# A hybrid Hyena/mLSTM encoder layer: the stores ahead of attention move from the SyncE queue to the GpSimd queue, and one landing tile is added

## The chip, the cores and the metric

One core of a Trainium2 chip. The time is device microseconds of one execution. Engines are named as the profile names them: PE is the matrix engine, DVE the vector engine, ACT the scalar engine, POOL is GpSimd, SP is SyncE, which computes nothing here and only issues DMA transfers. SPq is SP's own queue of instructions.

## The reference, cut to what matters

The layer takes x (2048 rows of 1024, float32) through one combined input projection and two parallel groups of heads, then an output projection, a cross-attention to 256 memory rows and a squared-ReLU MLP:

- the **Hyena group**: `z <- x1 * (h1 * z + d1 z); z <- x2 * (h2 * z + d2 z)`, two long convolutions ("orders" 0 and 1) with filters as long as the sequence, done by Fourier transforms, each followed by a gate; then a group norm.
- the **mLSTM group**: four heads of 128, exponential input gate, sigmoid forget gate, a running maximum, in chunks, once per direction. Its backward direction needs a state per chunk, which is carried from chunk to chunk.
- both go through `concat -> @ w_out -> + x`, then attention, then the MLP, then a final norm.

Everything is float32, and the comparison with the reference is at that precision; the large products run as three products of split operands.

## The kernel before, in words

**Stages.** The first 1170 us or so of the execution lie ahead of attention. They run in this order, woven into each other: the input projection in column "sweeps" with the filter generation beside it (to some 410 us); Hyena order 0 (recurrence over 16 blocks, to some 620 us); its inverse transform together with the forward transform of order 1 (to some 745 us); order 1's blocks (to some 960 us); order 1's inverse transform, called the tail here (to some 1110 us), with the projection of the memory (`memproj`, products L708, L725, L737) and the backward mLSTM states (`backward`, L1196, L1200, L1219) beside it; and the first five mLSTM steps (`mlstm`, L1284 to L1358). After that attention and the remaining eleven mLSTM steps run woven together, then the MLP.

**What passes through DRAM.** The stages hand their intermediate data to each other through DRAM, because the data has to change its layout. The stores that do this are the subject of the change:

- `by_phase` (L339) stores `fs` (filter spectra), `zs` (spectra of the signal) and loads `zg`; `back` (L989) stores `zg` (products of the block recurrence), always on POOL;
- `sweep_out` stores `hy` (L828, L834), `qt` and `kt` (L837) and `kn` (L849, L858); `natural` stores `vd`, `od` (L896, always on POOL) and the gates `gt` (L903);
- the gates store `rows` (L1161, L1162); the backward recurrence stores `cbd` (L1219); the tail stores `yh` (L1068); mLSTM stores `ym` (L1358); `memproj` stores `gd` and `vw` (L727, L739), always on POOL.

**What sets the order.** Every engine works its own queue in order; an instruction whose operand is not there holds everything behind it on that engine. The order of each queue is fixed when the program is built, by a scheduler with a cost model of its own, from the order of the code, so that moving an instruction to another queue can also move others. Transfers wait in two ways: for the data, and for a free place, since each of the two kinds of queue has eight completion counters that go round, so that a transfer waits for the one eight places earlier on its kind of queue. SP carries all big loads (weights, x, spectra), and before the change most of the stores as well.

**The block recurrence.** Block i of an order (loop at L1017) takes four loads: `em` (an inverse matrix, L949), `dm` (a forward matrix, L944), `fs` and `zs` (L920). PE multiplies `zs` by `dm` (L1030), DVE, ACT and POOL (L1035) combine it with the filter, PE multiplies by `em` (L987), and POOL stores the result to `zg`. The loads of block i+1 are asked for in block i. `em` has two buffers, so that the load for block i+1 has to wait until PE has finished L987 of block i-1. `zs`, `fs` and `zg` share ten buffers "a".

**The junk tile.** The mLSTM step squares its output on ACT (L1349) only for the sums that come with it (`accum_out`); the squares themselves go into a tile `junk` that nobody reads.

## Time and profile before

| | |
|---|---|
| median of 3 runs | 3070.66 us (3070.19 to 3076.88) |
| the profiled execution | 3074.8 us, span 3073.1 us, so 1.7 us lie around the span |
| instructions | 44126 |
| busy share of the span | PE 97%, PEld 77%, DVE 63%, ACT 49%, POOL 39% |
| mean granted PE clock | 0.988 |
| DMA | 607.03 MB, mean 198 GB/s |
| the chain that ended last | PE 82%, DMA 7%, DVE 5%, ACT 2%, POOL 1%, SPq 1% |

PE is busy for 2981.7 of 3073.1 us; the rest, 91.4 us, is all that a better order of waits could give, and 63.6 us of it lie in the first 1190 us. A wait row "A <- B: total, times, longest" gives the idle time of A that B ended. SP rows in these lists show how long SP stood at an instruction, and are only worth something if somebody waits for what stands behind it.

### The profile page before, as it was taken

The page shows a single profiled execution, that of the slowest core. Times are in us where ns is not written, and L with a number is a line of the kernel's source. Part 1 is how long each engine was busy: PE and PEld are TensorE (multiplying, and loading weights), DVE is VectorE, ACT ScalarE, POOL GpSimd, SP SyncE. Part 2 cuts the span into 40 slices and gives each one's busy share as a digit, 9 for nine tenths or more (in the row PEclk, how much of TensorE's full clock was granted, in tenths as well). Part 3 has the DMA queues.
Part 4 walks back from the last instruction along what each step waited for, and adds up shares of the span by engine and source line. Part 5 has one row for each costly group of instructions (what it writes and reads, how often), then busy time and mean ns, then how long its engine had stood idle before and what let it go on. Part 6 is the DMA issues. An engine that isn't in the chain of part 4 may idle for free.

```text
span 3073.1 us, 44126 instructions
## 1 busy us (share of the span) xinstructions
PE 2981.7 (97%) x14799; PEld 2367.8 (77%) x14799; DVE 1947.8 (63%) x3442; ACT 1491.4 (49%) x2930; POOL 1213.7 (39%) x942
## 2 busy tenths in 40 slices
PE   9999999998999898999999999999999999999998
PEld 7666667775678667888887888888888888888876
DVE  8855555556755547868665666558555676566695
ACT  6443455634754235555544455556555443333335
POOL 0112113310333544333133247765565374344653
PEclk9999999999999998999999999999999999999999
DMA  6655677586877986564567466657544565344434
GB/s 225 194 188 173 209 250 232 185 275 198 268 218 220 328 286 206 159 223 134 186 205 256 152 209 217 206 182 249 189 154 153 186 199 172 116 159 120 155 103 164
DMA packets 427867, 607.03 MB, mean 198 GB/s; under 512 B 38894, under 2 KB 232302, under 8 KB 426616
## 3 DMA queue, kind: packets, MB, share of 16 engines
q1 hardware_dynamic: 406644, 546.43, 55.6%
q0 software_dynamic: 12544, 41.95, 3.8%
q10 hardware_dynamic: 8452, 15.83, 1.4%
q8 instruction: 117, 1.92, 0.3%
q14 instruction: 110, 0.90, 0.1%
HBM read 401.67 MB, written 202.41 MB: 197 GB/s over the span
## 4 chain that ended last, share of the span: by engine, by line
PE 82%; DMA 7%; DVE 5%; issue 2%; ACT 2%; POOL 1%; SPq 1%; DVEq 0%; ACTq 0%; POOLq 0%
PE mm L355 17%; PE mm L358 17%; PE mm L359 17%; PE hy L359 6%; PE hy L355 6%; PE hy L358 6%; PE hy L173 2%; PE hy L1030 2%; PE mm L956 2%; PE hy L987 1%; DMA va<-vd 1%; DMA a<-zg 1%; PE hy L1322 1%; PE hy L1324 1%; PE mm L825 1%
## 5 line engine op out<-in xcount | busy, mean ns | idle before, releaser
L1692 ACT CAST ah<-w 128x512 fp32r<-128x512 f32 x284 | 176.5, 622 | 300.5 <-PE hy L358 155.9
L1693 DVE TENSOR_TENSOR bl<-wr,bh 128x512 fp32r<-128x512 f32 x213 | 240.0, 1131 | 125.4 <-ACT bh L1692 125.0
L366 DVE TENSOR_TENSOR wl<-wn,wh 128x512 fp32r<-128x512 f32 (+1 forms) x296 | 215.6, 772 | 90.9 <-ACT wh L366 90.6
L355 PE MATMUL mm<-xh,wh 128*128 128x512 f32 x640 | 266.6, 418 | 1.9 <-ACT xh L366 1.0
L358 PE MATMUL mm<-xl,wh 128*128 128x512 f32 x640 | 255.1, 399 | 4.6 <-DVE xl L366 4.6
L359 PE MATMUL mm<-xh,wl 128*128 128x512 f32 x640 | 254.4, 398 | 0.0
L1692 ACT CAST bh<-wr 128x512 fp32r<-128x512 f32 x232 | 143.6, 621 | 228.3 <-PE mm L359 174.3
L1693 DVE TENSOR_TENSOR al<-w,ah 128x512 fp32r<-128x512 f32 x236 | 217.4, 922 | 57.0 <-ACT ah L1692 57.0
L355 PE MATMUL mm<-bh,ah 128*128 128x512 f32 x576 | 225.8, 392 | 1.4 <-DVE acc L1854 1.3
L359 PE MATMUL mm<-bh,al 128*128 128x512 f32 x576 | 223.8, 391 | 3.4 <-DVE al L1693 3.4
L358 PE MATMUL mm<-bl,ah 128*128 128x512 f32 x576 | 224.9, 390 | 0.0
L366 ACT CAST wh<-wn 128x512 fp32r<-128x512 f32 (+1 forms) x296 | 164.6, 620 | 103.9 <-PE mm L359 50.1
L358 PE MATMUL mm<-act,wh 128*128 128x512 f32 x512 | 201.9, 394 | 0.0
L355 PE MATMUL mm<-act,wh 128*128 128x512 f32 x512 | 198.6, 394 | 1.4 <-ACT wh L366 1.3
L359 PE MATMUL mm<-act,wl 128*128 128x512 f32 x512 | 199.5, 392 | 0.1
L355 PE MATMUL hy<-bh,ah 128*128 128x512 f32 x448 | 175.2, 391 | 0.0
L358 PE MATMUL hy<-bl,ah 128*128 128x512 f32 x448 | 174.6, 390 | 0.0
L359 PE MATMUL hy<-bh,al 128*128 128x512 f32 x448 | 174.4, 390 | 0.0
L331 POOL TENSOR_TENSOR b<-b 128x512 f32<-128x512 f32 x32 | 48.1, 1504 | 293.3 <-DVE b L330 273.7
L355 PEld LDWEIGHTS mm<-xh,wh 128*128 128x128 f32 x640 | 121.6, 190 | 52.0 <-issue 21.2
L358 PEld LDWEIGHTS mm<-xl,wh 128*128 128x128 f32 x640 | 121.7, 190 | 51.3 <-issue 20.2
L355 PE MATMUL mm<-wh,xh 128*128 128x256 f32 (+1 forms) x512 | 155.1, 303 | 1.2 <-DVE a L960 1.2
(390 smaller groups left out, 8210.0 us busy)
## 6 DMA issues: line engine op xcount, KB each, us to landing
wr<-hc SPq DMA_DIRECT2D x224, 256.0 KB
w<-in_ff_w_dram SPq DMA_DIRECT2D x172, 256.0 KB
hc<-wn SPq DMA_DIRECT2D x128, 256.0 KB
wn<-in_w_in_dram SPq DMA_DIRECT2D x100, 256.0 KB
hc<-q SPq DMA_DIRECT2D x96, 256.0 KB
fs<-a SPq DMA_DIRECT2D x32, 512.0 KB
a<-fs SPq DMA_DIRECT2D x64, 256.0 KB
a<-zs SPq DMA_DIRECT2D x64, 256.0 KB
```

Of the source, the lines that this page charges most:

```text
L173: b = self.nc.tensor.matmul(*products[-1], start=True, stop=True)
L331: nc.gpsimd.tensor_tensor(b, f, b, ALU.subtract)
L355: first = mm(ps, lh, rh, start=start, stop=False)
L358: mm(ps, lh, rl, start=False, stop=False)
L359: self.last = mm(ps, ll, rh, start=False, stop=stop)
L366: both = (self.nc.scalar.copy(hi, src), self.nc.vector.tensor_tensor(lo, src, hi.bitcast(F32), ALU.subtract))
L825: nc.tensor.transpose(pt[0:w, jj], cv[:, 4 * j4 + jj:8 * w:8], self.ident)
L956: nc.tensor.matmul(pp, dm[:, m], t[:, m], start=True, stop=True)
L987: nc.tensor.matmul(pg, em[:, m], y, start=True, stop=True)
L1030: nc.tensor.matmul(pp, dm[:, m], t[:, m], start=True, stop=True)
L1692: self.nc.scalar.copy(hi, src)
L1693: eng.tensor_tensor(lo, src, hi.bitcast(F32), ALU.subtract)
```

## The change

Three things:

1. Every store listed above that SP issued is issued by POOL instead: `fs` 32, `hy` 60, `qt` and `kt` 16, `kn` 24, `gt` 2, the second half of `zs` 16, `rows` 2, `cbd` 15, `yh` 32 and `ym` 16, 215 transfers in all. POOL issued 144 before.
2. The `em` tile has three buffers instead of two (1 KB per partition each).
3. The `junk` tile is 128x128 instead of 128x4x128: the four squares of a step overwrite each other. This frees 1.5 KB per partition in a later pool.

```diff
@@ filters, front
-                    self.by_phase(nc.sync, sd[o], j2, h, st[h])
+                    self.by_phase(nc.gpsimd, sd[o], j2, h, st[h])
@@ sweep_out
-                nc.sync.dma_start(out=dst[:, 4 * j4:4 * j4 + 4], in_=st[0:w])
+                nc.gpsimd.dma_start(out=dst[:, 4 * j4:4 * j4 + 4], in_=st[0:w])
...
-                nc.sync.dma_start(out=self.d_hy[ct // 4, t0 + 8 * w:t0 + n, cc], in_=st[0:16, 0])
+                nc.gpsimd.dma_start(out=self.d_hy[ct // 4, t0 + 8 * w:t0 + n, cc], in_=st[0:16, 0])
...
-        nc.sync.dma_start(out=(self.d_qt if ct < 16 else self.d_kt)[h, :, t0:t0 + n], in_=v)
+        nc.gpsimd.dma_start(out=(self.d_qt if ct < 16 else self.d_kt)[h, :, t0:t0 + n], in_=v)
...
-                nc.sync.dma_start(out=self.d_kn[r0:r0 + 128 * full, cc].rearrange("(j q) c -> q j c", q=128),
+                nc.gpsimd.dma_start(out=self.d_kn[r0:r0 + 128 * full, cc].rearrange("(j q) c -> q j c", q=128),
...
-                nc.sync.dma_start(out=self.d_kn[t0 + s0:t0 + s0 + rest, cc], in_=st[0:rest, 0])
+                nc.gpsimd.dma_start(out=self.d_kn[t0 + s0:t0 + s0 + rest, cc], in_=st[0:rest, 0])
@@ natural
-                        nc.sync.dma_start(out=dst.rearrange("(t p) g -> p t g", p=128), in_=sg)
+                        nc.gpsimd.dma_start(out=dst.rearrange("(t p) g -> p t g", p=128), in_=sg)
@@ hyena
-            em = sb.tile([128, 2, 128], F32, tag="em", name="em", bufs=2)
+            em = sb.tile([128, 2, 128], F32, tag="em", name="em", bufs=3)
...
-                self.by_phase(nc.sync if h else nc.gpsimd, sds[o], j2, h, st[h])
+                self.by_phase(nc.gpsimd, sds[o], j2, h, st[h])
...
-                    nc.sync.dma_start(out=yh[q, :, js], in_=sq[phase[q]])
+                    nc.gpsimd.dma_start(out=yh[q, :, js], in_=sq[phase[q]])
@@ gates
-            nc.sync.dma_start(out=rows[0], in_=negM)
-            nc.sync.dma_start(out=rows[1], in_=inter)
+            nc.gpsimd.dma_start(out=rows[0], in_=negM)
+            nc.gpsimd.dma_start(out=rows[1], in_=inter)
@@ backward
-            self.nc.sync.dma_start(out=cbd[n - 1], in_=new.rearrange("d h e -> d (h e)"))
+            self.nc.gpsimd.dma_start(out=cbd[n - 1], in_=new.rearrange("d h e -> d (h e)"))
@@ mlstm
-            junk = sb.tile([128, 4, 128], F32, tag="h1", name="junk", bufs=1)
+            junk = sb.tile([128, 128], F32, tag="h1", name="junk", bufs=1)
...
-                nc.scalar.activation(junk[:, h], y[:, h], AF.Square, accum_out=ss[:, c:c + 1])
+                nc.scalar.activation(junk, y[:, h], AF.Square, accum_out=ss[:, c:c + 1])
...
-                    stores.append(lambda t0=t0, y=y: nc.sync.dma_start(
+                    stores.append(lambda t0=t0, y=y: nc.gpsimd.dma_start(
```

Line numbers are the same in both kernels. What the change moves in the queues is seen best at three places. The rows of a queue give its instructions in order: the line, the operation, `out<-in`, the shape, and a count where a row repeats.

**SP at the end of order 1's blocks.** `kn` and `va` are the backward recurrence's loads, `cbd` its stores, `qt` the query stores of the last column sweep, `zg` the tail's loads. Before:

```order
L1178 DMA kn<-kn 128x512
L1184 DMA va<-vd 128x4x128
L1219 DMA cbd<-cb 128x516
L837 DMA qt<-cv 128x1040 x2
L1178 DMA kn<-kn 128x512
L1184 DMA va<-vd 128x4x128
L1219 DMA cbd<-cb 128x516
L339 DMA a<-zg_2739 128x1024 x2
L974 DMA a<-hy 32x1024 x4
```

and now:

```order
L1178 DMA kn<-kn 128x512
L1184 DMA va<-vd 128x4x128
L1178 DMA kn<-kn 128x512
L1184 DMA va<-vd 128x4x128
L1178 DMA kn<-kn 128x512
L1184 DMA va<-vd 128x4x128
L339 DMA a<-zg_2739 128x1024 x2
L974 DMA a<-hy 32x1024 x4
```

The `qt` and `cbd` stores that stood between the loads have gone from SP.

**POOL in the tail.** L1060 and L1066 are the tail's squares and gains, L1196 the backward recurrence's weighted values, `gd` the stores of memproj, L1290 works for the mLSTM steps. Before:

```order
L1060 TENSOR_TENSOR a<-a 128x1024
L1290 TENSOR_TENSOR rw<-rw,qn 128x512 x3
L727 DMA gd<-o 128x2x256
L1066 TENSOR_TENSOR a<-a,ghy 128x512 x2
L727 DMA gd<-o 128x2x256 x2
L1060 TENSOR_TENSOR a<-a 128x1024
L727 DMA gd<-o 128x2x256
L1196 TENSOR_TENSOR va<-va,cols 128x516
```

and now:

```order
L727 DMA gd<-o 128x2x256 x3
L1066 TENSOR_TENSOR a<-a,ghy 128x512 x2
L1219 DMA cbd<-cb 128x516
L727 DMA gd<-o 128x2x256
L1068 DMA yh<-a 32x1024 x4
L1060 TENSOR_TENSOR a<-a 128x1024
L727 DMA gd<-o 128x2x256
L1196 TENSOR_TENSOR va<-va,cols 128x516
```

Four `yh` stores and a `cbd` store now stand in POOL's queue between one L1066 and the next L1060.

**PE at the first mLSTM steps.** L708 and L737 are products of memproj; L1284, L1322, L1324 and L1200 belong to the mLSTM steps. Before:

```order
L708 MATMUL mm<-mt,wm 128x256 x9
L737 MATMUL mm<-wm,kt 128x512 x8
L1284 MATMUL hy<-qn,kk_t 128x128 x8
L708 MATMUL mm<-mt,wm 128x256 x10
L1322 MATMUL hy<-va,rw 128x129 x5
...
L708 MATMUL mm<-mt,wm 128x256 x6
L737 MATMUL mm<-wm,kt 128x512 x4
L1200 MATMUL hy<-ve,kn 128x129 x4
L737 MATMUL mm<-wm,kt 128x512 x2
L1284 MATMUL hy<-qn,kk_t 128x128 x4
```

and now:

```order
L708 MATMUL mm<-mt,wm 128x256 x10
L737 MATMUL mm<-wm,kt 128x512 x10
L1284 MATMUL hy<-qn,kk_t 128x128 x8
L737 MATMUL mm<-wm,kt 128x512 x6
L1322 MATMUL hy<-va,rw 128x129 x5
...
L1200 MATMUL hy<-ve,kn 128x129 x4
L1284 MATMUL hy<-qn,kk_t 128x128 x4
```

Of 16 L708 and 16 L737 that stood behind the first L1284, only 6 L737 still do; the others now stand ahead of it. From the attention stage on PE's order is the same in both kernels.

## The prediction

> **What bounds the kernel now.** I read first the busy shares and the queues on the page of the profile, then a table of busy time by stage, then the waits of PE, and only then those of SP.
>
> ```profile
> PE 2981.7 (97%) x14799; PEld 2367.8 (77%) x14799; DVE 1947.8 (63%) x3442; ACT 1491.4 (49%) x2930; POOL 1213.7 (39%) x942
> q1 hardware_dynamic: 406644, 546.43, 55.6%
> q0 software_dynamic: 12544, 41.95, 3.8%
> ```
>
> PE is the bound: 97% of 3073.1 us. The stores of POOL are the software queue q0, 3.8% of the DMA engines' time; everything that SP issues is in q1. The columns of the next view are stretch, length, busy time of PE, PEld, DVE, ACT and POOL, granted clock, share of the DMA engines, GB/s.
>
> ```profile
> 0.00:410.00 410.00, 397.82 (x2262) 282.25 (x2263) 266.05 (x489) 202.93 (x347) 52.78 (x45) 0.99 0.62 205
> 410.00:630.00 220.00, 212.49 (x1148) 159.58 (x1148) 133.42 (x205) 135.44 (x243) 74.60 (x81) 0.98 0.68 212
> 630.00:745.00 115.00, 103.81 (x677) 72.18 (x675) 66.02 (x195) 39.48 (x70) 7.26 (x12) 0.96 0.81 259
> 745.00:960.00 215.00, 208.34 (x967) 148.77 (x968) 136.67 (x224) 131.39 (x225) 76.79 (x81) 0.98 0.71 216
> 960.00:1110.00 150.00, 137.73 (x793) 110.76 (x792) 67.45 (x187) 39.84 (x80) 65.69 (x63) 0.98 1.00 324
> 1110.00:1190.00 80.00, 66.26 (x350) 52.00 (x349) 49.25 (x166) 41.97 (x149) 38.95 (x36) 0.89 0.67 218
> 1190.00:3073.00 1883.00, 1855.31 (x8610) 1542.30 (x8609) 1228.93 (x1978) 900.32 (x1819) 897.62 (x624) 1.00 0.55 177
> ```
>
> PE stands idle for 12.2, 7.5, 11.2, 6.7, 12.3 and 13.7 us in the six stretches ahead of attention, 63.6 in all. That is the whole stake. Only in the tail, 960 to 1110, are the DMA engines full (1.00); there, and at the start of the mLSTM steps behind it, is the place to look. The waits of PE, in total, times and longest:
>
> ```profile
> PE hy L1030 <- DMA a<-zs: 8.8, 3, 4.4
> PE mm L725 <- ACT kt L710: 5.8, 2, 4.2
> PE hy L173 <- DMA a<-zg: 2.8, 2, 2.3
> PE hy L1200 <- POOL va L1196: 1.8, 1, 1.8
> ```
>
> and of SP's queue:
>
> ```profile
> SPq L949 <- PE hy L987: 113.7, 20, 13.9
> SPq L339 <- ACT a L311: 77.2, 25, 11.5
> SPq L828 <- ACT st L201: 55.2, 21, 5.8
> SPq L837 <- ACT cv L801: 23.0, 3, 11.2
> ```
>
> So SP stands for 113.7 us at `em` loads and 155.4 us at the three kinds of store listed, but PE waits for a transfer of what stands behind only 11.6 us in all (8.8 for `zs`, 2.8 for `zg`). Most of SP's waiting is covered by loads that were asked for a block ahead.
>
> **The change part by part.**
>
> *Stage entries.* The first `zs` load of an order cannot go until the last `zs` store has landed. SP and POOL around the two entries:
>
> ```profile
> 413.99 0.34 SPq L339 DMA_DIRECT2D zs<-a  x1
> 416.83 1.17 SPq L920 DMA_DIRECT2D a<-zs  x2
> 740.28 0.33 SPq L339 DMA_DIRECT2D zs<-a  x1
> 745.24 1.17 SPq L920 DMA_DIRECT2D a<-zs  x2
> ...
> zs<-a POOLq DMA_DIRECT2D x16, 512.0 KB, 6.2
> ```
>
> On SP the store is followed by the load after 2.84 us at the first entry, and after 4.96 us at the second, where five other stores stand between. A POOL `zs` store takes 6.2 us to land at the median. By that the entries would lose 3.4 and 1.2 us; if SP's wait were all that counts, they would gain up to the 8.8 us. PE waits there anyway, so each microsecond counts. I take 0: the five stores that go and the slower landing about cancel.
>
> *The third `em` buffer.* PE's idle time inside the block recurrences is 7.5 and 6.7 us, of which the waits for `zs` at the entries explain the larger part; no wait of L987 for `em` and none of L1030 for `fs` stands among PE's waits. The cover is the loads of a block ahead. I price it at 0; with the cover gone it would be some of the 14.2 us.
>
> *SP at the end of order 1.* Here SP really holds back loads while the DMA engines are not full:
>
> ```profile
> 941.30 11.87 SPq L837 DMA_DIRECT2D qt<-cv  x2
> 953.70 0.32 SPq L1178 DMA_DIRECT2D kn<-kn  x1
> 958.09 0.79 SPq L339 DMA_DIRECT2D a<-zg  x2
> 953.69 0.53 POOL L989 DMA_DIRECT2D zg<-a  x1 [3.62 <-ACT a L988]
> ...
> zg<-a POOLq DMA_DIRECT2D x64, 256.0 KB, 4.2
> ...
> 940.00:950.00 10.00, 10.00 (x40) 7.21 (x39) 7.24 (x12) 7.23 (x11) 4.82 (x5) 1.00 0.39 136
> 950.00:960.00 10.00, 10.00 (x52) 8.24 (x51) 4.23 (x14) 2.82 (x4) 1.64 (x3) 1.00 0.70 191
> ```
>
> The second `qt` store waits to 953, and the loads behind it meet a full queue afterwards. Unused DMA time in these 20 us: 6.1 + 3.0 = 9.1 us, the upper bound of the gain. But the `zg` loads that open the tail go out at 958.09 because the last `zg` store, issued at 953.69, lands 4.2 us later; that doesn't move. Only `kn`/`va` pairs can use the gap, of 512 KB each, at the tail's 324 GB/s 1.6 us. Two of them earlier are 3 us. I take -3, bounds -9.1 and 0.
>
> *POOL's own cost.*
>
> ```profile
> L1035 POOL TENSOR_TENSOR b<-b,a 128x512 f32<-128x512 f32 x64 | 88.7, 1386 | 104.9 <-ACT b L1033 90.7 <-issue 10.5 <-DVE a L960 3.1
> L989 POOL DMA_DIRECT2D zg<-a x64 | 35.9, 561 | 110.6 <-ACT a L988 56.1 <-PE hy L1030 26.9 <-DVE b L1036 10.5
> L896 POOL DMA_DIRECT2D vd<-st x16 | 11.9, 745 | 34.7 <-ACT st L891 34.7
> ```
>
> An issue with one row per partition takes 0.56 us (`zg`), with two 0.745 us (`vd`), so about 0.18 for each further one. Of the 215 stores 64 (`hy`, `kn`) have four pieces a partition, an estimate of 1.1 us; the other 151 are at most like `zg`. That is 70 + 85 = 155 us, on an engine busy for 39%. What counts is what stands behind a store that has to wait: L1035, L1196, L1060 and L1066. In the tail 32 `yh` stores (18 us) and a part of `cbd` join 65.69 busy us of 150, so POOL stays under two thirds. Each group of four `yh` stores puts the next L1060 back by 2.2 us, eight groups 18 us if all of it lay on the path; nothing, if the full DMA engines set the pace. The only PE wait that points at POOL there is the 1.8 us. I take +1, bounds 0 and +18.
>
> *The work that moved on PE.* Of memproj's products 16 L708 and 10 L737 now stand ahead of the first L1284 and no longer between the first steps. Each product makes two records in the trace:
>
> ```profile
> L737 PE MATMUL mm<-wm,kt 128*128 128x512 f32 x34 | 15.4, 592 | 0.0
> L708 PE MATMUL mm<-mt,wm 128*128 128x256 f32 x32 | 7.2, 379 | 0.0
> L1322 PE MATMUL hy<-va,rw 128*128 128x129 f32 x64 | 12.7, 292 | 7.4 <-DVE ht L1356 4.3 <-DVE bry L213 3.1
> ...
> 1130.00:1140.00 10.00, 10.00 (x60) 7.35 (x59) 6.73 (x19) 8.06 (x28) 4.14 (x5) 1.00 0.41 137
> 1140.00:1150.00 10.00, 9.79 (x48) 6.25 (x47) 3.97 (x16) 7.85 (x30) 9.28 (x10) 1.00 0.69 203
> 1150.00:1160.00 10.00, 2.83 (x16) 2.67 (x17) 7.39 (x29) 2.74 (x12) 2.64 (x3) 0.71 0.84 302
> ```
>
> The first rows are PE's groups from 1115 to 1175. All of L708 (7.2 us) and 20 of the 34 records of L737 (9.1 us) go: 16.3 us. They were the cover under which the chain over ACT, DVE and POOL of the first steps ran; from 1150 to 1160, where no more of it was left, PE did 2.83 us of work. The tail ahead has 12.3 idle us to take them in, so at least 4 us stay over; how much of the cover was needed the trace doesn't say. Bounds 0 (all taken in, the chain no longer) and +16.3 (none taken in, the chain as long as now). The tail's idle time being of the same size speaks for the lower part: +2.
>
> *The rest.* Early sweeps: PE's idle 12.2 us there are waits for DVE and ACT, none for a load; 0. `ym`: PE's idle time from 1190 on is 28 us, its order is unchanged; 0. `junk`: four squares on one engine, in order; 0.
>
> Sum: 0 + 0 - 3 + 1 + 2 = 0. The profiled execution (3074.8 us) stays at 3074.8; it lies 4.1 us above the median of 3070.66, so the sum in medians is 3070.7. I lean by 2 us to the lower side, since the two large negative bounds (-8.8 and -9.1) belong to waits that the trace shows, and the positive ones to delays that I only infer: **3068.7 us**. A difference under 0.2%, 6.1 us, can hardly be told from none.
>
> The Trainium skill, "DMA: Bandwidth & Descriptors", section "Issuing engines are not separate DMA queues", says that starting DMAs on more engines saves only the sequencer's time for starting them. By it the sum would be 0 for the tail too, since the trace shows the DMA engines full there; the gap from 941 to 953 is head-of-line waiting, of which the section says nothing.
>
> **The rivals.**
>
> *A real gain, 3057.* SP without stores lets each load go as soon as its buffer is free. If the whole gap of 9.1 us is used and half of the waits for `zs` (4.4) goes: 3070.7 - 13.5 = 3057. For it: SP's 11.87 us hold and the share of 0.39. Against it: the `zg` loads hang on their own store.
>
> *The lost cover, slower, 3083.* The 16.3 us of products moved ahead of the first mLSTM steps are not taken in by the tail, because there they wait for weights on full DMA engines (1.00) or for ACT (the 5.8 us at L725), and the steps then run as long as before with PE idle: 3070.7 + 16.3 - 3 = 3084, with a little taken in 3083. It decides as soon as PE's idle time from 1110 on grows by more than the tail's shrinks. For it: PE at 2.83 of 10 us where the cover ended. Against it: PE fully busy from 1130 to 1140, in the midst of the first steps, so the cover was not all needed.
>
> *POOL's issues grow under DVE.*
>
> ```profile
> L1693 DVE TENSOR_TENSOR bl<-wr,bh 128x512 fp32r<-128x512 f32 x213 | 240.0, 1131 | 125.4 <-ACT bh L1692 125.0
> ```
>
> If each issue were held up by the vector instruction beside it, whose costliest group takes 1.1 us, 215 issues would take 240 us more, and POOL would reach 39% + 5% + 8% = 52%; with half of the tail's 18 us on the path, 3080. The `zg` rows speak against it: 561 ns over 64 issues, while DVE is busy for 136.67 of the 215 us of order 1's stage.
>
> The Trainium skill, "SBUF — State Buffer", section "SBUF: two separate sides", has this as a trap: GpSimd cannot write descriptors while VectorE holds the shared port. The `zg` rows show no trace of it.
>
> **How the numbers follow.** No change but for a few microseconds: 0.36 (0.27 within 0.2%, 0.07 faster, 0.02 slower). A real gain: 0.31. The lost cover: 0.26. POOL under DVE: 0.04, slower. That the change does nothing at all, since all of SP's waiting is covered: 0.03, same. So faster 0.38, same 0.30, slower 0.32. The likeliest case by itself spans 3063 to 3076. The range reaches to the gain's 3057 and some way past it, since its bounds add up to -18, and to the lost cover's 3083: 3053 to 3084.
>
> **What would show it.** Right: the tail's DMA share at 940 to 960 rises and `kn`/`va` loads stand there; PE's waits for `zs` stay near 8.8 us; the block recurrences keep their length; POOL's issue rows stay at 0.55 to 0.75 us, `hy` near 1.1; PE's idle time from 1110 to 1190 grows and that of 960 to 1110 shrinks by about as much. Wrong: L1035 or L1060 waiting behind stores so that L987 or L173 name POOL; a tail shorter by more than 6 us; a wait of attention's first products for `yh`.

## The result, and the profile after

The changed kernel takes 3087.39 us at the median of 8 runs (3078.88 to 3095.39), the kernel before 3072.50 us (3070.19 to 3076.88). The ratio is 1.0041 with a 95% interval of 1.0030 to 1.0053: slower by some 12.6 us (the medians are 14.9 us apart, inside the interval of 9.2 to 16.3). A few executions that took far longer than the others of their kernel (8414.7 us in one of `yh` and `cbd` alone, 3738.1 in one of `kn`, `kt` and `qt` alone, 3336.11 in one of the kernel before) are left out of all ratios. The profiled execution took 3086.58 us, 11.8 us more than that of before, and its span is 11.8 us longer too. The forecast was no change (3068.7 us), and the time lies outside its range.

The busy shares and the software queue of the changed kernel:

```profile
PE 2986.8 (97%) x14799; PEld 2370.9 (77%) x14799; DVE 1943.9 (63%) x3442; ACT 1496.7 (49%) x2930; POOL 1350.9 (44%) x1157
q0 software_dynamic: 31472, 104.92, 9.2%
```

POOL has 215 more instructions and is busy for 137 us more; the queue q0 carries 104.92 MB instead of 41.95. PE has the same 14799 instructions, but is busy for 2986.8 us where it was 2981.7. So of the 11.8 us 6.7 are longer waits of PE, and 5.1 are the same work done more slowly, at a mean granted clock of 0.985 where it was 0.988 (the last section comes back to this). The same stretches as before tell roughly where the waits are (PE, PEld, DVE, ACT, POOL, granted clock, share of the DMA engines, GB/s):

```profile
0.00:410.00 410.00, 394.36 (x2248) 279.85 (x2256) 263.75 (x486) 200.36 (x344) 112.80 (x137) 0.99 0.60 203
410.00:630.00 220.00, 210.76 (x1142) 157.05 (x1135) 132.65 (x204) 135.39 (x242) 86.49 (x97) 0.98 0.67 212
630.00:745.00 115.00, 104.57 (x689) 73.26 (x688) 67.07 (x192) 38.75 (x65) 18.12 (x29) 0.94 0.79 255
745.00:960.00 215.00, 204.84 (x941) 143.49 (x941) 137.12 (x222) 133.44 (x232) 93.89 (x109) 0.98 0.68 214
960.00:1110.00 150.00, 144.23 (x821) 117.81 (x820) 64.00 (x180) 41.59 (x81) 81.92 (x98) 0.98 0.99 328
1110.00:1190.00 80.00, 60.48 (x297) 45.14 (x295) 46.06 (x153) 38.51 (x136) 45.79 (x48) 0.83 0.60 196
```

PE's idle time is now 15.6, 9.2, 10.4, 10.2, 5.8 and 19.5 us; before it was 12.2, 7.5, 11.2, 6.7, 12.3 and 13.7. The tail has less of it, the first mLSTM steps have more, and so have three of the four stages ahead. Stretches of fixed borders mix a delay with the work that it pushes over the border, though. A cleaner reading takes the same instruction in both traces:

| instruction | before, us | after, us | later by |
|---|---|---|---|
| L331 on POOL, the last (filter generation) | 341.5 | 341.9 | 0.4 |
| L1030, the first (order 0's blocks begin) | 420.3 | 424.0 | 3.7 |
| L1035, number 32 (order 0's blocks end) | 617.0 | 620.5 | 3.5 |
| L1035, number 33 (order 1's blocks begin) | 752.2 | 756.9 | 4.7 |
| L1035, number 64 (order 1's blocks end, the tail begins) | 944.9 | 953.2 | 8.2 |
| L1284, the first (mLSTM steps begin) | 1115.6 | 1131.7 | 16.1 |
| L1479, the first (attention begins) | 1170.3 | 1183.4 | 13.1 |
| L1942 (in the MLP), the last | 2534.6 | 2543.5 | 8.9 |
| the end of the span | 3073.1 | 3084.9 | 11.8 |

So nothing is lost up to the end of the filters; 3.5 us at the entry to order 0; about 1.2 us up to order 1 and 3.5 us inside its blocks; 4.9 us in the tail and the first steps together (+7.9, then -3.0). From attention on 4.2 us are won back and 2.9 lost again. Each column is one execution: a kernel that has only the new buffer and the small tile, and takes the same time as before, has its marks 1.4 us earlier at the beginning of the tail and 3.7 us earlier at the last L1942, so that differences of that size say little.

PE's order from attention on, called the same in both kernels further up, differs in small swaps up to 1446 us. The kernel with only the buffer and the small tile has such swaps too (119 places), and they cost it nothing that can be measured.

The waits of PE and of SP that changed most:

```profile
PE hy L1030 <- DMA a<-zs: 10.4, 2, 6.1
PE hy L1322 <- DVE den L1330: 5.0, 1, 5.0
PE hy L1322 <- DVE bry L213: 3.3, 1, 3.3
PE hy L1200 <- ACT ht L1336: 3.0, 3, 2.1
...
SPq L949 <- PE hy L987: 140.9, 22, 13.9
SPq L395 <- DVE wl L366: 188.4, 48, 26.4
SPq L1178 <- PE hy L1200: 65.7, 17, 15.6
```

These waits of the mLSTM steps (L1322, L1200) for DVE and ACT are new or longer. SP no longer stands at these stores, but it stands longer at its loads: the time at `em` loads went from 113.7 to 140.9 us, at weights (L395) from 63.7 to 188.4, at `kn` (L1178) from 38.4 to 65.7. It also stands until stores of POOL have landed: 72.6 us at loads of the filter generation (L292 <- DMA `fs`; 9.8 before) and 25.1 us at the `zs` loads (2.7 before). What SP had waited for at the stores it now waits for at the loads. The weights (L395) go out 2.6 us later at the median of 104 loads; the `em` loads go out 7.5 us earlier (32 loads), but no wait of PE had asked for that.

The entry to order 0, SP's loads and POOL's stores:

```profile
415.67 0.53 POOL L339 DMA_DIRECT2D zs<-a  x1 [1.01 <-DVE a L998]
...
419.78 1.18 SPq L920 DMA_DIRECT2D a<-zs  x2
```

The `zs` load now goes 4.11 us after the last store (2.84 us before, when that store was on SP) and at 419.78 instead of 416.83 us. PE waits 6.1 us for it; it was 3.3. In PE's queue four instructions fewer stand ahead of the first L1030 than before, so it is the later load that goes with these 2.8 us. At order 1's entry the wait is what it was, 4.3 us (4.4 before).

### The profile page after: what moved, and what is told of

The parts are those of the page before. It is cut to its first block, busy times and chain, and to the rows that moved or that the text cites. A ratio compares the mean times of both kernels' runs of the same rounds, so it can differ in the third digit from the quotient of the medians.

```text
span 3084.9 us, 44197 instructions
## 1 busy us (share of the span) xinstructions
PE 2986.8 (97%) x14799; PEld 2370.9 (77%) x14799; DVE 1943.9 (63%) x3442; ACT 1496.7 (49%) x2930; POOL 1350.9 (44%) x1157
## 3 DMA queue, kind: packets, MB, share of 16 engines
q0 software_dynamic: 31472, 104.92, 9.2%
## 4 chain that ended last, share of the span: by engine, by line
PE 57%; DVE 3%; DMA 1%; issue 1%; ACT 1%; POOL 0%; SPq 0%; DVEq 0%; POOLq 0%; ACTq 0%
PE mm L355 12%; PE mm L359 12%; PE mm L358 12%; PE hy L355 6%; PE hy L359 6%; PE hy L358 6%; PE hy L1322 1%; PE hy L1324 1%; DVE bl L1693 0%; PE hy L1284 0%; PE hy L1596 0%; DVE acc L1991 0%; PE hy L1200 0%; DVE acc L2028 0%; PE hy L1479 0%
## 5 line engine op out<-in xcount | busy, mean ns | idle before, releaser
L355 PE MATMUL mm<-xh,wh 128*128 128x512 f32 x640 | 266.2, 417 | 4.3 <-ACT xh L366 2.5
L358 PE MATMUL mm<-xl,wh 128*128 128x512 f32 x640 | 255.3, 399 | 3.5 <-DVE xl L366 3.5
L359 PE MATMUL mm<-xh,wl 128*128 128x512 f32 x640 | 253.6, 397 | 0.0
L359 PE MATMUL mm<-bh,al 128*128 128x512 f32 x576 | 224.1, 392 | 4.1 <-DVE al L1693 4.1
L355 PE MATMUL mm<-bh,ah 128*128 128x512 f32 x576 | 226.3, 393 | 0.5 <-DVE acc L1854 0.4
L358 PE MATMUL mm<-bl,ah 128*128 128x512 f32 x576 | 225.2, 391 | 0.0
L358 PE MATMUL mm<-act,wh 128*128 128x512 f32 x512 | 201.8, 394 | 0.0
L355 PE MATMUL mm<-act,wh 128*128 128x512 f32 x512 | 199.0, 395 | 0.8 <-ACT act L366 0.5
L359 PE MATMUL mm<-act,wl 128*128 128x512 f32 x512 | 199.4, 391 | 0.0
L355 PE MATMUL hy<-bh,ah 128*128 128x512 f32 x448 | 175.2, 391 | 0.0
L358 PE MATMUL hy<-bl,ah 128*128 128x512 f32 x448 | 174.6, 390 | 0.0
L359 PE MATMUL hy<-bh,al 128*128 128x512 f32 x448 | 174.4, 390 | 0.0
L355 PEld LDWEIGHTS mm<-xh,wh 128*128 128x128 f32 x640 | 121.4, 190 | 55.7 <-issue 23.4
L358 PEld LDWEIGHTS mm<-xl,wh 128*128 128x128 f32 x640 | 121.3, 189 | 46.7 <-issue 18.0
L355 PE MATMUL mm<-wh,xh 128*128 128x256 f32 (+1 forms) x512 | 154.7, 302 | 1.2 <-DVE a L960 1.2
L359 PE MATMUL hy<-x,al 128*128 128x512 f32 x384 | 149.5, 389 | 1.6 <-DVE al L1693 1.6
```

What stands on the lines that cost most here:

```text
L355: first = mm(ps, lh, rh, start=start, stop=False)
L358: mm(ps, lh, rl, start=False, stop=False)
L359: self.last = mm(ps, ll, rh, start=False, stop=stop)
```

## The experiments

All compare with the kernel before on the same chip; every run but the last is a comparison in five rounds, with a 95% interval. Two readings of the traces go with them: PE's wait ahead of the first L1030 (the entry to order 0), and the time from order 1's last L1035 over the first L1284 to the first L1479 ("tail", "steps").

My theory after the result was: stores on POOL cost at the entries (`zs`), inside order 1's blocks (`kn`), and in the tail and the first steps through the order of PE that comes with `yh` and `cbd` there. The rivals: the third `em` buffer; POOL's longer queue in the tail; the cover being all of it (the cover, or filling, is work that PE does while it would otherwise have to wait).

### The buffer alone

```diff
-            em = sb.tile([128, 2, 128], F32, tag="em", name="em", bufs=2)
+            em = sb.tile([128, 2, 128], F32, tag="em", name="em", bufs=3)
...
-            junk = sb.tile([128, 4, 128], F32, tag="h1", name="junk", bufs=1)
+            junk = sb.tile([128, 128], F32, tag="h1", name="junk", bufs=1)
...
-                nc.scalar.activation(junk[:, h], y[:, h], AF.Square, accum_out=ss[:, c:c + 1])
+                nc.scalar.activation(junk, y[:, h], AF.Square, accum_out=ss[:, c:c + 1])
```

> The kernel before with the third em buffer and the small junk tile alone, all stores as before. Theory (the loss lies in stores that go through POOL): within 3 us of before, since no PE wait names em. Rival (the third buffer lets SP send loads earlier than the stores they compete with): 4 to 8 us slower, and the first L1030 of order 0 later than 420.3 us. Second rival: the SP waits of 113.7 us at em were worth something: 4 us or more faster.

Ratio 0.9998 (0.9986 to 1.0011). The buffer and the small tile are worth nothing and cost nothing that can be measured, with the stores on SP.

### `yh` and `cbd` alone on POOL

```diff
-                    nc.sync.dma_start(out=yh[q, :, js], in_=sq[phase[q]])
+                    nc.gpsimd.dma_start(out=yh[q, :, js], in_=sq[phase[q]])
...
-            self.nc.sync.dma_start(out=cbd[n - 1], in_=new.rearrange("d h e -> d (h e)"))
+            self.nc.gpsimd.dma_start(out=cbd[n - 1], in_=new.rearrange("d h e -> d (h e)"))
```

> The kernel before with the yh and cbd stores alone on POOL. This alone puts 26 memproj products ahead of the first L1284, as in the change. Theory (cover lost): the tail up to the first L1284 grows by some 8 us, the first mLSTM steps shrink by only 3 us, 5 us slower in all. Rival (what costs is early, at the zs entries and in order 1's recurrence): within 2 us of before.

Ratio 1.0018 (1.0009 to 1.0027), 5.6 us slower. Tail 177.2 us (before 170.7), steps 53.4 (54.8): +6.5 and -1.4. The order of PE differs from before only near the tail and the steps. But the stores and PE's order change together here, so it does not tell which of them costs. The next one changes the order with the stores where they were.

### Memproj's products ahead of the steps, all stores on SP

All stores stay on SP. The first four L1284 are held behind what stands ahead of them in the program, and memproj is written wholly ahead of the steps:

```diff
-                nc.tensor.matmul(sp[:, h], kk_t[:, h], qn[:, h], start=True, stop=True)
+                (tc.keep_in_program_order if n == 0 else lambda i: i)(nc.tensor.matmul(sp[:, h], kk_t[:, h], qn[:, h], start=True, stop=True))
...
-            for _ in chain(p.turned_in(), take(n, 1), beside_each(n, take(m, 5))):
+            for _ in chain(p.turned_in(), take(n, 1), n, take(m, 5)):
```

> The kernel before, all stores on SP, with all memproj products ordered ahead of the first L1284 (16 L708 and 16 L737 more ahead of it). Theory (the cover counts, whoever issues the stores): first L1284 some 8 to 10 us later, the steps from there to the first L1479 a few us shorter, 5 to 8 us slower in all. Rival (POOL's longer queue in the tail is what costs, not PE's order): within 2 us of before.

Ratio 1.0026 (1.0015 to 1.0038), 8 us slower, with not a store on another queue. The tail takes 193.2 us (+22.5, where 8 to 10 were expected), the steps 41.3 (-13.5, where "a few" were). All 32 products moved, 6 more than in the change, and ACT, DVE and SP follow with some new order of their own. The products taken out of the steps weigh 22.2 us (L737 15.0, L708 7.2), and the tail took none of them into its idle time, which is 13.1 us (12.3 before). So the steps did get shorter, but by less than their filling weighs: the products that stood among them ran in time that the steps need anyway for ACT, DVE and POOL. PE's groups in the steps of this kernel:

```profile
L1322 PE MATMUL hy<-va,rw 128*128 128x129 f32 x64 | 13.2, 301 | 5.0 <-DVE bry L213 2.6 <-DVE ht L1356 1.8 <-DVE rw L1294 0.6
L1200 PE MATMUL hy<-ve,kn 128*128 128x129 f32 x32 | 6.6, 369 | 5.6 <-ACT ht L1336 5.6
```

The 5.6 us at L1200 for ACT were 0.5 before. The rival that POOL's queue is what costs in the tail is not needed: memproj's place alone costs as much as, or more than, `yh` and `cbd` on POOL, where fewer products moved (0.26% against 0.18%, with intervals that overlap). That POOL's queue costs nothing at all there is not shown.

### The second half of `zs` alone on POOL

```diff
-                self.by_phase(nc.sync if h else nc.gpsimd, sds[o], j2, h, st[h])
+                self.by_phase(nc.gpsimd, sds[o], j2, h, st[h])
```

> The kernel before with the second half of the zs stores alone on POOL. Theory (a later and slower landing of the last zs store holds the first zs load): the first zs load of order 0 goes 2 to 3 us later than 416.83, that of order 1 some 0 to 4 us later than 745.24, 3 to 5 us slower in all. Rival (the entries are late only because stages ahead of them are late): within 2 us of before.

Ratio 0.9982 (0.9972 to 0.9991), 5.5 us **faster**. Both theory and rival fall. The first `zs` load does go later, at 420.04 instead of 416.83 us, 3.99 us after its store, as the theory said. But PE does not wait for it: its wait ahead of the first L1030 is nothing, where it was 3.3 us. In PE's queue 28 more instructions (25 rows) stand ahead of the first L1030, 24 products of the column sweeps (L355, L358, L359) and four transposes (L845). The build put them there because of the move. Order 1's load goes earlier, at 739.51 instead of 745.24 us, and its blocks begin 5.8 us earlier: 2.0 of these are there at the end of order 0's blocks, and between the two the gates' wait at L1134 is 2.7 us (3.6 before) and the last products of the forward transform (L186) run at 732.3 instead of 738.3 us.

### The change without `yh` and `cbd`

They stay on SP; all else is the change. This brings back the 26 memproj products behind the first L1284.

```diff
-                    nc.gpsimd.dma_start(out=yh[q, :, js], in_=sq[phase[q]])
+                    nc.sync.dma_start(out=yh[q, :, js], in_=sq[phase[q]])
...
-            self.nc.gpsimd.dma_start(out=cbd[n - 1], in_=new.rearrange("d h e -> d (h e)"))
+            self.nc.sync.dma_start(out=cbd[n - 1], in_=new.rearrange("d h e -> d (h e)"))
```

> The change without its yh and cbd stores, which stay on SP; memproj's products then stand behind the first L1284 as before. Theory (two separate losses: some 8 us ahead of 860 us, from stores in the stages up to there, and some 5 us from the lost cover): L1035 number 57 still 7 to 9 us later than 895.6 us, first mLSTM steps no further behind, 6 to 8 us slower in all. Rival (the cover is the whole loss and the early delay would be caught up later): within 2 us of before.

Ratio 1.0022 (1.0013 to 1.0030), 6.8 us slower than before. About as the theory said: L1035 number 57 comes 9.3 us later than before (7 to 9 were expected), tail and steps together take 222.8 us (225.4 before, 230.3 in the change). The cover is one of two losses; the delay ahead of 860 us is the other and isn't caught up.

### `hy` alone on POOL

```diff
-                nc.sync.dma_start(out=dst[:, 4 * j4:4 * j4 + 4], in_=st[0:w])
+                nc.gpsimd.dma_start(out=dst[:, 4 * j4:4 * j4 + 4], in_=st[0:w])
...
-                nc.sync.dma_start(out=self.d_hy[ct // 4, t0 + 8 * w:t0 + n, cc], in_=st[0:16, 0])
+                nc.gpsimd.dma_start(out=self.d_hy[ct // 4, t0 + 8 * w:t0 + n, cc], in_=st[0:16, 0])
```

> The kernel before with the hy stores alone on POOL. Theory (hy stores, 0.8 us of POOL each and in between the last zs stores, make order 0's or order 1's entry late): first L1030 of order 0 or of order 1 2 to 4 us later than 420.3 and 751.5 us, 2 to 4 us slower. Rival (kn and kt are what costs): within 2 us of before.

Ratio 0.9999 (0.9990 to 1.0007). Sixty stores, the costliest group of them for POOL (38.6 us for 48), cost nothing that can be measured. The theory's part on `hy` falls.

### `kn`, `kt` and `qt` alone on POOL

```diff
-        nc.sync.dma_start(out=(self.d_qt if ct < 16 else self.d_kt)[h, :, t0:t0 + n], in_=v)
+        nc.gpsimd.dma_start(out=(self.d_qt if ct < 16 else self.d_kt)[h, :, t0:t0 + n], in_=v)
...
-                nc.sync.dma_start(out=self.d_kn[r0:r0 + 128 * full, cc].rearrange("(j q) c -> q j c", q=128),
+                nc.gpsimd.dma_start(out=self.d_kn[r0:r0 + 128 * full, cc].rearrange("(j q) c -> q j c", q=128),
...
-                nc.sync.dma_start(out=self.d_kn[t0 + s0:t0 + s0 + rest, cc], in_=st[0:rest, 0])
+                nc.gpsimd.dma_start(out=self.d_kn[t0 + s0:t0 + s0 + rest, cc], in_=st[0:rest, 0])
```

> The kernel before with the kn, kt and qt stores alone on POOL. Theory (kn stores share the st tiles and POOL's queue with L1035 and hold PE's transposes in the block recurrence): order 1's blocks, from the first L1030 to the last, take some 3 us longer than 191.4 us, 3 to 5 us slower in all. Rival (hy or fs): within 2 us of before.

Ratio 1.0007 (0.9996 to 1.0018): no difference that can be told, though the interval (-1.2 to +5.5 us) does not rule out the 3 us of the theory. How long its stages take is read from a second trace, see below.

### `fs` alone on POOL

```diff
-                    self.by_phase(nc.sync, sd[o], j2, h, st[h])
+                    self.by_phase(nc.gpsimd, sd[o], j2, h, st[h])
```

> The kernel before with the fs stores alone on POOL. Theory (they have their cover: fs is loaded a block ahead, and POOL is nearly idle then): within 2 us of before. Rival (POOL's later issue holds the a tiles, so that the filter generation and the loads of the decay windows are late): 3 us or more slower, and L331's last at 344 us or later instead of 341.5.

Ratio 1.0013 (1.0003 to 1.0023), some 4 us slower. The rival's size, but not its mechanism: the last L331 runs at 340.1 us, not later than the 341.5 of before. The delay is spread: 0.8 us at order 0's blocks, 3.0 at the start of order 1's, 3.5 at the first L1284. PE's order is another one in the filter generation, from 136 to some 350 us, then again from some 740 us. I found no single wait that carries the delay.

### The change without `kn`, `kt` and `qt`

The same lines back to SP.

> The change without its kn, kt and qt stores, which stay on SP (yh, cbd, fs and the rest on POOL). Theory (kn stores on POOL cost order 1's recurrence about 4 us): from the first L1035 of order 1 (number 33 of 64) to its last the time is 192.7 us as before and not 196.3 as in the change; 3 to 5 us faster than the change, so 7 to 9 us slower than before. Rival (the stretch is lost to the other stores there, or to the third em buffer): the stretch stays near 196 us.

Ratio 1.0024 (1.0014 to 1.0033). Against the change's 1.0041 this is 5 us better, and the blocks of order 1 take 192.0 us instead of 196.3. By itself this supports the theory; the last two runs put it right.

### The change without `fs`

The one line back to SP.

> The change without its fs stores, which stay on SP. Theory (fs alone on POOL cost 4 us and the losses add): 3 to 5 us faster than the change, about 8 us slower than before. Rival (what fs cost alone came from the order that the build chose with it, and does not add): like the change, 11 to 14 us slower than before.

Ratio 1.0013 (1.0003 to 1.0022): 4 us slower than before and 8.6 us better than the change, more than twice what `fs` cost alone. So the losses do not add; but the rival's 11 to 14 us fall as well. The trace tells why: PE's wait for the first `zs` load is gone (6.1 us in the change), although the load goes at 419.41, hardly earlier than in the change (419.78). The first L1030 has the same 28 instructions more ahead of it as with `zs` alone; in the change it has four fewer than before. With `fs` on POOL too, the build leaves out of the entry the products that it had put there for the later `zs` load.

### What is left when the costly stores stay on SP

`zs`, `hy`, `gt`, `rows`, `cbd` and `ym` on POOL, with the buffer and the small tile; `fs`, `kn`, `kt`, `qt` and `yh` on SP.

```diff
-                    self.by_phase(nc.gpsimd, sd[o], j2, h, st[h])
+                    self.by_phase(nc.sync, sd[o], j2, h, st[h])
...
-        nc.gpsimd.dma_start(out=(self.d_qt if ct < 16 else self.d_kt)[h, :, t0:t0 + n], in_=v)
+        nc.sync.dma_start(out=(self.d_qt if ct < 16 else self.d_kt)[h, :, t0:t0 + n], in_=v)
...
-                    nc.gpsimd.dma_start(out=yh[q, :, js], in_=sq[phase[q]])
+                    nc.sync.dma_start(out=yh[q, :, js], in_=sq[phase[q]])
```

(and the two `kn` lines).

> The change without fs, kn, kt, qt and yh on POOL: zs, hy, gt, rows, cbd and ym on POOL, with the third em buffer and the small junk tile; memproj's products stand as before. Theory (what costs is fs, kn and kt, and yh through PE's order; zs gains): 3 to 7 us faster than before, like the zs stores alone. Rival (every further store on POOL costs something): at or above before.

Ratio 0.9990 (0.9981 to 0.9999), 3 us faster: the theory's lower end. The rival (at or above before) falls, if narrowly.

### The last memproj products further back

With `zs` alone on POOL, eight L737 are put behind the second step:

```diff
-                        mul(p, t[:, m, ms], o_[:, m, ds], start=m == 0, stop=m == 1)
+                        (self.tc.keep_in_program_order if h == 3 else lambda i: i)(mul(p, t[:, m, ms], o_[:, m, ds], start=m == 0, stop=m == 1))
...
-            for _ in chain(p.turned_in(), take(n, 1), beside_each(n, take(m, 5))):
+            for _ in chain(p.turned_in(), take(n, 8), take(m, 3), n, take(m, 2)):
```

> The kernel with the zs stores alone on POOL, and of memproj's last products eight L737 moved further back, behind the second mLSTM step's L1200. Theory (the cover counts where PE would stand idle, and there is idle time behind the third step): from the first L1284 to the first L1479 some 2 to 4 us shorter than 53.8 us. Rival (where the cover stands among the steps does not matter as long as it stands behind the first L1284): within 1 us of 53.8.

Ratio 0.9999 (0.9990 to 1.0008), so the gain of `zs` alone is lost. The steps take 59.3 us, not 53.8: both expectations fall. The move also put 16 L708 and 6 L737 between the first and the second L1284, and the second group of L1284 came 13 us after the first, where with `zs` alone the two stand back to back. It isn't the edit that I meant to make; all it shows is that where the filling stands among the steps counts for several microseconds, in either direction.

### The two pieces of PE's order given back together

The change with only `fs`, `yh` and `cbd` back on SP; `zs`, `hy`, `kn`, `kt`, `qt`, `gt`, `rows` and `ym`, 136 of the 215 stores, stay on POOL.

```diff
-                    self.by_phase(nc.gpsimd, sd[o], j2, h, st[h])
+                    self.by_phase(nc.sync, sd[o], j2, h, st[h])
...
-                    nc.gpsimd.dma_start(out=yh[q, :, js], in_=sq[phase[q]])
+                    nc.sync.dma_start(out=yh[q, :, js], in_=sq[phase[q]])
...
-            self.nc.gpsimd.dma_start(out=cbd[n - 1], in_=new.rearrange("d h e -> d (h e)"))
+            self.nc.sync.dma_start(out=cbd[n - 1], in_=new.rearrange("d h e -> d (h e)"))
```

> The change without its fs, yh and cbd stores, which stay on SP; zs, hy, kn, kt, qt, gt, rows and ym on POOL, third em buffer, small junk tile. In its queue on PE 23 more rows stand ahead of the first L1030 than in the change, and memproj's products stand behind the first L1284 as before. Theory (the loss is the work that PE's new order took out of two waits, at order 0's entry and at the first mLSTM steps): no wait of PE for the first zs load, tail and steps together near 223 us instead of 230.3, and 3 us slower to 4 us faster than before in all. Rival (kn, kt and qt on POOL cost some 5 us by themselves): 3 us or more slower than before, and order 1's blocks near 196 us.

Ratio 0.9986 (0.9977 to 0.9995): 4.3 us **faster** than before. The theory's numbers hold (the gain is at the edge of the 4 us): no wait for the first `zs` load, tail and steps 224.0 us. Of the waits of PE from 400 to 440 us this is all that is left, and PE's busy time there (second number) is full where the change had 6.03 of 10 us:

```profile
PE mm L355 <- DVE st L203: 0.4, 1, 0.4
PE mm L845 <- ACT P L788: 0.2, 1, 0.2
...
420.00:430.00 10.00, 10.00 (x43) 6.91 (x42) 5.83 (x12) 5.76 (x11) 4.97 (x6) 1.00 0.96 280
```

The same stretch in the change, and then before:

```profile
PE hy L1030 <- DMA a<-zs: 6.1, 1, 6.1
...
420.00:430.00 10.00, 6.03 (x13) 3.45 (x14) 4.00 (x9) 4.25 (x8) 2.68 (x3) 0.66 0.72 230
```

```profile
PE hy L1030 <- DMA a<-zs: 3.3, 1, 3.3
...
420.00:430.00 10.00, 9.73 (x36) 7.11 (x37) 2.79 (x6) 2.23 (x4) 1.28 (x1) 0.83 0.54 158
```

And the rival falls: with `kn`, `kt` and `qt` on POOL the kernel is faster than before, though order 1's blocks take 195.3 us. The second run gives their trace alone:

> The same kernel as with kn, kt and qt alone on POOL, for its trace. Theory (kn on POOL stretches order 1's blocks): first to last L1035 of order 1 some 196 us. Rival (that stretch is not from kn): 191.5 to 195 us, as in the kernels that leave kn on SP.

The blocks of order 1 take 195.5 us, 2.8 more than before; but tail and steps take 166.1 and 55.5 us, together 3.8 less. What the blocks lose is given back in the tail. Kernels that leave `kn` and `kt` on SP have 191.6 to 195.1 us in the blocks, those with them on POOL 194.5 to 197.7, so that part of the 2.8 us is the spread of the builds.

Four of these kernels make a square, in ratios to the kernel before, all with `zs`, `hy`, `kn`, `kt`, `qt`, `gt`, `rows` and `ym` on POOL:

| | `yh`, `cbd` on SP | `yh`, `cbd` on POOL |
|---|---|---|
| `fs` on SP | 0.9986 | 1.0013 |
| `fs` on POOL | 1.0022 | 1.0041 |

`yh` and `cbd` cost 0.27% and 0.19%, `fs` 0.36% and 0.28%; the intervals are about 0.1% to each side. The two together take the kernel from 0.14% faster to 0.41% slower, 17 us: that is the whole of the loss. The places agree: with `fs` on POOL PE's order changes between 136 and some 900 us (and in a few places behind 1200), with `yh` and `cbd` only from some 950 us on. Fastest of all was `zs` alone (0.9982), which can't be told from the kernel with 136 stores on POOL (0.9986); both beat the kernel before and the change.

What stays open: the 0.36% of `fs` are some 11 us, read in the two traces of the left column. The wait for `zs` at the entry is 5.5 us with `fs` on POOL and nothing with it on SP, and at the end of order 0's blocks the kernel with `fs` on POOL is 3.1 us behind. A further 6.4 us lie between order 0's blocks and order 1's (137.44 us from the last L1035 of the one to the first of the other, against 131.07), and 2.4 us in order 1's blocks; these are not traced to one wait, so the mechanism of most of what `fs` costs is not shown. At the entry many builds agree: with the second half of `zs` on POOL the load goes between 418.5 and 421.2 us, and PE waits 5.1 to 6.1 us in the three with `fs` on POOL, and nothing in the five with `fs` on SP. So it is PE's order that decides whether the later load costs anything. Against the kernel before, whose order there is nearly the change's, the change loses by the later load, and lacks the filling that the other builds have. No run changed those rows of PE alone.

## Why the prediction was wrong, point by point

Two terms of the sum failed. The early stores were put at 0, and `fs` costs 0.28 to 0.36%, 9 to 11 us; the work that moved on PE was put at +2, and `yh` and `cbd`, with which it moves, cost 0.19 to 0.27%, 6 to 8 us. The step behind both is that the prediction took PE's order and its waits as given everywhere but at the first mLSTM steps, while the move changed what PE has to do ahead of its waits from 136 us on. For `fs` this is seen at order 0's entry alone, in builds that agree; the rest of its cost stays open.

- **What bounds the kernel, and that SP's waits are covered: right.** SP no longer stood for 155.4 us at stores, and the change gained nothing from it; SP then stood longer at its loads.
- **The third `em` buffer, 0: right** (0.9998).
- **POOL's own cost: right in kind, too high in size.** The issues cost (count, busy us, mean ns):

```profile
L828 POOL DMA_DIRECT2D hy<-st x48 | 38.6, 806 | 130.2 <-ACT st L201 120.9 <-DVE st L203 7.2 <-issue 1.0
L989 POOL DMA_DIRECT2D zg<-a x64 | 36.2, 566 | 94.2 <-ACT a L988 55.8 <-PE hy L1030 25.5 <-DVE b L1036 8.8
L339 POOL DMA_DIRECT2D fs<-a x32 | 17.9, 560 | 41.1 <-ACT a L311 40.7 <-issue 0.4
L849 POOL DMA_DIRECT2D kn<-st x16 | 12.4, 776 | 12.5 <-DVE b L1034 5.1 <-DVE st L203 4.4 <-ACT st L201 3.0
```

  A store of four pieces a partition takes 0.8 us where 1.1 was estimated; all together some 137 us against 155. The 19 us less for the 64 stores of `hy` and `kn` are of no consequence, as `hy` alone shows. `zg` at 566 ns (561 before) says that its issues did not grow beside DVE: that rival had no part in it. The trap of which the Trainium skill's page "SBUF — State Buffer", section "SBUF: two separate sides", warns does not show in these rows.
- **SP at the end of order 1, -3: wrong in its mechanism.** The gap did not fill. SP's queue and the stretches around it in the change, which runs 8 us later here:

```profile
945.70 0.52 SPq L1184 DMA_DIRECT2D va<-vd  x1
961.94 0.33 SPq L1178 DMA_DIRECT2D kn<-kn  x1
...
940.00:950.00 10.00, 10.00 (x46) 7.74 (x45) 6.88 (x14) 4.57 (x6) 4.73 (x5) 1.00 0.37 107
950.00:960.00 10.00, 10.00 (x41) 7.19 (x40) 7.17 (x10) 6.75 (x12) 4.15 (x6) 1.00 0.39 132
```

  SP now stands at the `kn` load, for 16 us, until PE has used the buffer (L1178 <- PE L1200). The same load goes 8.8 us after the last L1035 of order 1 in both kernels (953.70 after 944.9, 961.94 after 953.2), and in both just behind the products L1200 that begin at 952.6 and 960.9. So the `qt` store had hidden a wait that was there anyway: removing the wait that ended last showed the next.
- **Stage entries, 0: right in kind, too small, and wrong for PE.** The load goes 3 us later at order 0's entry, near the +3.4 that the prediction had worked out and then set off against the five stores that go; PE's wait grew by 2.8 us there, and not at order 1's entry. The prediction took PE's wait as given ("PE waits there anyway, so each microsecond counts"). It isn't: what PE has in its queue ahead of L1030 differs between the builds, and makes a load at about the same time cost 5 to 6 us or nothing. The prediction looked at PE's order only at the mLSTM steps, though the first difference in PE's queue comes at 136 us.
- **The work that moved on PE, +2 with bounds 0 and +16.3: right mechanism, too small.** It measured +4.9 in the change's tail and steps, and 0.19 to 0.27% (6 to 8 us) by the square, in which the stores move with it. The wrong part is the argument that the tail's 12.3 idle us would take the products in: it took in 6.5 us (idle 5.8 us after), and the steps gave back 3.0 us of the 16.3 that had gone.
- **The early stores, 0: wrong for `fs`.** "PE's idle 12.2 us there are waits for DVE and ACT, none for a load" was true of the stage in which `fs` is stored; by the marks the cost comes later.
- **"The block recurrences keep their length": not for order 1.** Its blocks take 196.3 us instead of 192.7. No term of the sum had this, and no run shows one cause for it.
- **The rivals.** The lost cover was right by sign and by mechanism, but it is less than half of the loss: 4.9 us where it was priced at some 12. That its 3083 us come near the 3087 is luck, as the rest of the loss is of another kind. A gain was found in a part of the change, `zs` (3067 us), but not by that rival's mechanism, in which loads go out earlier: order 0's first `zs` load goes 3.2 us later, and PE has more work ahead of it.
- The Trainium skill's page "DMA: Bandwidth & Descriptors", section "Issuing engines are not separate DMA queues", says that starting DMAs on more engines saves only the sequencer's time. `hy` (0.9999) and `kn`, `kt` and `qt` (1.0007) agree with it, and so do the 155.4 us of SP's waits at stores that bought nothing. The 5.5 us of `zs` came with another order of PE, of which the section says nothing.

## What to carry to other kernels

Where a scheduler orders the queues, moving an instruction is two edits: the move, and the new order of everything else. Compare the whole queue of the bounding engine, at each place where it waits for something, before pricing the move. Where a gain or a cost could be traced here, it was mostly a matter of which spare work stands ahead of a wait. And a change of many like edits is worth splitting: here 136 of 215 moved stores gain 4 us and the other 79 lose 17.

## What the runs showed that I had not expected

In these traces the granted clock of PE is lower where PE has just waited, and the work behind the wait runs slower. In the change, around the first steps (busy time of PE second, granted clock third from the end):

```profile
1150.00:1160.00 10.00, 5.96 (x25) 5.43 (x25) 7.51 (x21) 9.44 (x36) 2.50 (x2) 0.50 0.63 208
1160.00:1170.00 10.00, 5.89 (x25) 5.38 (x25) 6.14 (x27) 2.15 (x11) 1.86 (x2) 0.67 0.25 79
1170.00:1180.00 10.00, 7.88 (x48) 7.58 (x49) 7.20 (x26) 6.89 (x28) 6.71 (x6) 0.64 0.51 166
1200.00:1210.00 10.00, 10.00 (x59) 8.70 (x58) 4.54 (x18) 6.62 (x26) 6.31 (x5) 1.00 0.70 231
```

The products of the steps show it in their duration. A product of L1322 takes 275 ns at the median from 1115 to 1150 us, where the granted clock is 0.99 to 1.00, and 422 ns from 1150 to 1163 us, of which the first 10 us have a granted clock of 0.50. In the change more of them fall into such stretches: L1322 takes 329 ns at the mean, before 292.

```profile
L1322 PE MATMUL hy<-va,rw 128*128 128x129 f32 x64 | 14.8, 329 | 10.4 <-DVE den L1330 5.0 <-DVE bry L213 3.3 <-ACT ve L1194 1.2
```

Over the 64 records that is 2.1 us beside the 3.0 us by which the idle time ahead of them grew. So filling a wait is worth somewhat more than the wait. At order 0's entry the granted clock from 420 to 430 us goes the same way, with the lines shown above: 1.00 without a wait for `zs`, 0.83 with 3.3 us of it, 0.66 with 6.1. Over the whole span PE is busy for 5.1 us more with the same instructions, beside 6.7 us more of waits; that the clock is all of these 5.1 us is not shown.
